# Page numbers of a paged cache: four by one register load, bounded once for the whole table

## The chip, the cores and the metric

The kernel runs on one core of a Trainium2 chip. The metric is the device time of one execution in microseconds (us). The profile is of one execution, taken by the hardware profiler; its engines are PE (TensorE matmuls), PEld (weight loads), DVE (VectorE), ACT (ScalarE), POOL (GpSimd) and SP (SyncE), and SP here computes nothing: it loads registers and issues DMAs, in the order of its own instruction stream.

## What the kernel computes

One inference step of a two-layer decoder trunk, for a prompt of 1,040 tokens and for 8 samples of 4 new tokens each. Layer 0 is a convolution module and a ConvFFN; then a shared latent key/value side is computed; layer 1 is multi-head latent attention and a ConvFFN. The part that matters here is the attention of the samples over a paged cache:

```python
page_table = jax.random.permutation(key, n_phys)[:n_used].reshape(DEC_BATCH, n_pages)   # (8, 16) int32, n_phys = 160

def step(carry, phys):                    # scanned over the 16 pages of every sample
    m, l, acc = carry
    c = cache_lat[phys]                   # (8, 128, 128): one page of each sample
    kr = cache_kr[phys]                   # (8, 128, 32)
    k = key_nope(c, w_uk, knorm_nope)     # rms_norm of c @ w_uk, per head
    s = (q_nope . k + q_rope . kr) * SM_SCALE
    ...                                   # running softmax over s, acc += p . c
```

So 128 pages are read, each at an address that depends on a number in `page_table`. The norms of the keys need `c @ w_uk` of every page too.

## The kernel before

The program is written out in full (no loops on the chip). A planner orders the instructions of each engine by simulated times of readiness and by priorities; inside `manual_schedule(engines={X})` the order in which the code emits the instructions of engine X is kept among themselves. All loads named below are issued by SP, whose instructions run one after another; a DMA whose buffer is not yet free holds back everything behind it on SP.

The cache is read twice, each time as 32 groups of four pages, by the helper `pages(pt, slot, moves)` (L569). For each of the four pages it loads one int32 of the table (`pt`, a tile of 1 x 128 in SBUF) into a register of SP with `value_load` (L573), which also emits a check of the number against 0 and 159, and then issues one DMA whose source address is computed from the register (L575). `between` and `more` let other DMAs (L348) be put behind single pages at the very start.

- `cache_open` and `cache_norms` (L580 to L632), from the start of the kernel on: the first 128 columns of each page (`ct`, 64 KB a page) are brought in, split in a high and a low part (`ch` on ACT, `cl` on DVE or POOL), multiplied by `w_uk` on PE (L616) and squared and summed, as filler between the matmuls of the convolution module. `ct` has two buffers of four pages. At the very start the eight `x` tiles of the residual stream (L348) are loaded between the pages; the first weights `raw<-pw` (L155) come later on the same queue.
- `latents` (L910 to L1057) opens the second part: it loads the table again (L927, L928).
- `samples` (L1453 to L1652): the attention of the samples, in four pairs of samples `sp` = 0 to 3. `scores(sp)` has `fetch` (L1528) bring in 8 groups of four pages of the pair (`pg`, 192 KB a page: latent transposed, latent, rope key), from two pools of 8 tiles that the pairs take in turn; it splits them on ACT and DVE (L134, L1558, L135, L1559), multiplies on PE (L150, L1573) and combines on DVE (L1575, L1579). `values(sp)` does the softmax on ACT (L1592), transposes (L1603) and multiplies with the pages (L1614). `values(sp)` and `scores(sp + 1)` are interleaved step by step (L1636 to L1642). Before each pair a tile of key norms, `rk`, comes on the same queue (L1539).
- The first pair's scores are worked between the matmuls of the prompt's attention (L1297 to L1330); the second pair's pages go to memory that the prompt's attention gives back at its end (L1330). After `samples` come `project` (L1654) and the second ConvFFN.

Of the kernel before, what the change touches and what calls it, by code (L numbers as in the profile page):

```python
# [11 lines left out]
I32 = mybir.dt.int32  # L12
ALU = mybir.AluOpType
# [95 lines left out]
class Pair:  # L109
    def __init__(self, pools, n=0):  # L110
        self.pools, self.n = pools, n
# [6 lines left out]
class Prog:  # L118
    def __init__(self, tc, a, o):
        self.tc, self.nc, self.a, self.o = tc, tc.nc, a, o  # L120
        self.gate, self.between, self.help, self.wedge = [], [], 0, []

    def pool(self, es, name, bufs, side="left", **k):
        return es.enter_context(self.tc.tile_pool(name=name, bufs=bufs, side=side, reuse_waits="tile", **k))
# [414 lines left out]
    def layer_norm(self, ys):  # L539
# [26 lines left out]
        with self.tc.high_priority(PRIO):  # L566
            return self.rows_rstd(t, sums, T0)

    def pages(self, pt, slot, moves):  # L569
        nc = self.nc  # L570
        with self.tc.manual_schedule(engines={nc.sync.engine}):
            for j in range(4):
                pg = nc.sync.value_load(pt[0:1, slot + j:slot + j + 1], min_val=0, max_val=159)  # L573
                for t, src in moves:
                    last = nc.sync.dma_start(t[:, j], src(bass.ds(pg, 1)))  # L575
                if self.between:
                    self.more(self.between.pop(0))
        return last

    def cache_open(self, es):  # L580
        nc, a = self.nc, self.a
        self.kp = kp = self.pool(es, "kp", 2, "right")
        k1 = self.pool(es, "k1", 1, "right")
        self.pk = self.pool(es, "pk", 2, "right", space=PSUM)
        self.ks = self.pool(es, "ks", KS, "right")
        raw = self.wp.tile([128, 1024], F32, name="raw")
        self.ukh, self.ukl = k1.tile([128, 1024], F32R, name="ukh"), k1.tile([128, 1024], F32R, name="ukl")
        nc.sync.dma_start(raw, a["wuk"])
        self.split(self.ukh, self.ukl, raw)
        self.pt = k1.tile([1, 128], I32, name="pt")  # L590
        nc.sync.dma_start(self.pt, a["pt"])
        self.ss = k1.tile([128, 128, H], F32, name="ss")
        self.fill, self.pks, self.halve = self.cache_norms(), [], HALVE
        self.on_pool = ()
# [315 lines left out]
    def latents(self, es, eq, xh, xl, sq):  # L910
        nc, a, o = self.nc, self.a, self.o
        ac = self.pool(es, "ac", 1, "right")
# [11 lines left out]
        self.qs = ac.tile([128, H, NS], F32, name="qs")  # L924
        self.kr8 = ac.tile([32, 64], F32, name="kr8")
        self.cn8 = ac.tile([64, CL], F32, name="cn8")
        self.pt = ac.tile([1, 128], I32, name="pt")  # L927
        nc.sync.dma_start(self.pt, a["pt"])  # L928
        tabs = {}
        cs = {n: self.cst(n).rearrange("p (a b) -> p a b", b=16) for n in ("cos", "sin")}  # L930
        with ExitStack() as e2:
# [923 lines left out]
```

## Time and profile before

| | us |
|---|---|
| median of 3 runs (lowest to highest) | 2805.16 (2804.45 to 2807.96) |
| the profiled execution | 2805.34 |
| its span (first to last instruction) | 2803.6 |

The span is what the trace covers; the profiled execution is 1.7 us longer than it. In the rows, L573 is line 573 of the kernel, `SPq` is SP's instruction stream, "x8" is a count, and a row of a timeline or a chain begins with its start and its duration in us. A row of the page's section on DMA issues ends with the KB of one DMA and the median us from issue to landing.

### The profile page before, as it was taken

To read this page: it belongs to the slowest core of one execution; us is meant where nothing else is said; L and a number is where in the kernel's file an instruction comes from. 1 tells how busy PE (TensorE), PEld (TensorE's weight loads), DVE (VectorE), ACT (ScalarE), POOL (GpSimd) and SP (SyncE) were. 2 spreads that over 40 slices of the span, in tenths; PEclk is the share of its full clock that TensorE was granted. 3 is DMA by queue.
4 is the path that set the end of the run, shared out by engine and by line. 5 is a ranking of instruction groups with operands and counts; after the bars stand their busy time and mean duration, and the time that the engine had idled before them with its cause. 6 is when DMAs were issued, how large, how long until landed. Compare 5 with 4: busy or idle time off the path is not lost.

```text
span 2803.6 us, 47232 instructions
## 1 busy us (share of the span) xinstructions
PE 2664.4 (95%) x16934; PEld 2451.2 (87%) x16934; DVE 1889.1 (67%) x3526; ACT 1357.2 (48%) x3730; POOL 680.4 (24%) x988
## 2 busy tenths in 40 slices
PE   7999996999999999999789999988999999999999
PEld 5888875999999999999667676655999999999999
DVE  8899996478888774144776867665468777776131
ACT  6777775345445452023655565555235445444020
POOL 1467661033333330001211212100004333331000
PEclk9999997999999999999999999977999999999999
DMA  4111110503222235132101001357402222227122
GB/s 137 56 41 57 54 38 16 178 25 101 86 94 87 84 127 207 42 102 77 39 8 34 16 20 54 93 159 234 163 32 72 84 82 72 87 80 264 40 86 75
DMA packets 127776, 238.29 MB, mean 85 GB/s; under 512 B 39778, under 2 KB 81140, under 8 KB 127412
## 3 DMA queue, kind: packets, MB, share of 16 engines
q1 hardware_dynamic: 103828, 200.82, 22.2%
q0 software_dynamic: 9600, 32.36, 3.1%
q10 hardware_dynamic: 14112, 2.09, 0.5%
q8 instruction: 133, 2.18, 0.3%
q14 instruction: 103, 0.84, 0.1%
HBM read 183.90 MB, written 51.31 MB: 84 GB/s over the span
## 4 chain that ended last, share of the span: by engine, by line
PE 83%; DVE 7%; ACT 4%; issue 2%; DMA 2%; SPq 2%; POOL 0%; ACTq 0%; DVEq 0%; POOLq 0%
PE ps L758 29%; PE ps L174 22%; PE pk L616 5%; PE g L410 4%; PE v L1297 4%; PE ps L807 3%; PE p L150 2%; PE ps L196 2%; PE ps L976 1%; PE p L1307 1%; PE p L1309 1%; PE p L1310 1%; PE s L1267 1%; PE ps L150 1%; PE po L1614 1%
## 5 line engine op out<-in xcount | busy, mean ns | idle before, releaser
L134 ACT ACTIVATE wh<-raw 128x512 fp32r<-128x512 f32 (+2 forms) x256 | 191.1, 750 | 543.0 <-PE ps L174 341.4
L135 DVE TENSOR_TENSOR wl<-raw,wh 128x512 fp32r<-128x512 f32 (+2 forms) x244 | 201.4, 828 | 109.1 <-ACT wh L134 103.1
L904 DVE TENSOR_TENSOR x<-ps,x 128x1074 f32<-128x1074 f32 (+1 forms) x48 | 61.0, 1270 | 289.7 <-PE ps L174 289.7
L728 DVE SCALAR_TENSOR_TENSOR c<-ub,c,c 128x1040 f32<-128x1040 f32 (+1 forms) x176 | 225.5, 1314 | 30.0 <-ACT c L725 29.2
L631 ACT ACTIVATE qq<-pk 128x64 f32<-128x64 f32 x760 | 164.4, 244 | 74.9 <-PE pk L616 74.9
L723 POOL COPY sb<-ub 128x32 f32<-128x32 f32 x88 | 88.2, 1005 | 403.4 <-DVE ub L769 364.8
L1297 PE MATMUL v<-pf,vf 128*128 128x512 f32 (+4 forms) x448 | 175.6, 475 | 9.7 <-ACT pf L1314 9.2
L625 POOL TENSOR_TENSOR sq<-sq 128x256 f32<-128x256 f32 (+3 forms) x234 | 141.2, 608 | 104.3 <-ACT sq L620 95.9
L631 ACT ACTIVATION_READ_ACCUMULATOR qq<-pk 128x1 f32 x760 | 159.8, 228 | 0.2
L1314 ACT ACTIVATE pf<-p 128x512 f32<-128x512 f32 (+4 forms) x224 | 99.6, 451 | 121.7 <-DVE p L1312 101.0
L508 DVE SCALAR_TENSOR_TENSOR a<-u,c,a 128x512 f32<-128x512 f32 x216 | 151.2, 751 | 6.1 <-ACT a L501 6.1
L174 PE MATMUL ps<-xh,wh 128*128 128x358 f32 (+1 forms) x672 | 147.7, 328 | 7.1 <-ACT xh L134 5.4
L174 PE MATMUL ps<-xl,wh 128*128 128x358 f32 (+1 forms) x672 | 147.4, 327 | 0.1
L174 PE MATMUL ps<-xh,wl 128*128 128x358 f32 (+1 forms) x672 | 147.4, 327 | 0.0
L174 PE MATMUL ps<-al,wh 128*128 128x358 f32 (+1 forms) x672 | 147.2, 327 | 0.0
L174 PE MATMUL ps<-ah,wl 128*128 128x358 f32 (+1 forms) x672 | 146.5, 326 | 0.0
L174 PE MATMUL ps<-ah,wh 128*128 128x358 f32 (+1 forms) x672 | 146.2, 326 | 0.0
L616 PE MATMUL pk<-ukh,ch 128*128 128x512 f32 x256 | 112.3, 439 | 27.3 <-ACT ch L134 14.0
L725 ACT ACTIVATE c<-ub,c 128x1074 f32<-128x1074 f32 (+1 forms) x88 | 101.3, 1185 | 66.3 <-DVE ub L769 53.1
L174 PEld LDWEIGHTS ps<-xh,wh 128*128 128x128 f32 x672 | 116.7, 190 | 10.4 <-ACT xh L134 6.3
L620 ACT ACTIVATE sq<-pk 128x512 f32<-128x512 f32 x161 | 98.2, 616 | 46.4 <-PE pk L616 43.6
L134 ACT ACTIVATE wh<-s 128x512 fp32r<-128x512 f32 x120 | 75.7, 630 | 92.9 <-PE ps L758 86.3
(588 smaller groups left out, 9093.0 us busy)
## 6 DMA issues: line engine op xcount, KB each, us to landing
raw<-wup SPq DMA_DIRECT2D x88, 512.0 KB, 3.5
pg<-ctn SPq DMA_DIRECT2D x128, 192.0 KB, 2.6
raw<-wdn SPq DMA_DIRECT2D x32, 448.0 KB, 3.3
raw<-pw SPq DMA_DIRECT2D x24, 512.0 KB, 3.7
d_a<-c POOLq DMA_DIRECT2D x22, 537.0 KB, 3.5
raw<-d_a SPq DMA_DIRECT2D x22, 537.0 KB, 4.8
d_a<-c POOLq DMA_DIRECT2D x22, 531.0 KB, 3.1
raw<-d_a SPq DMA_DIRECT2D x22, 531.0 KB, 5.1
```

The lines of the kernel that those rows point to most:

```text
L134: return (nc.scalar.activation(h, src, AF.Copy), (eng or nc.vector).tensor_tensor(out=l, in0=src, in1=h.bitcast(F32), op=ALU.subtract))
L135: (eng or nc.vector).tensor_tensor(out=l, in0=src, in1=h.bitcast(F32), op=ALU.subtract))
L174: nc.tensor.matmul(p[:, c, :ch], s[:, k * 128:(k + 1) * 128], m[k][:, off + c * ch:off + (c + 1) * ch], start=k == 0 and i == 0, stop=k == ...
L410: y = nc.tensor.matmul(p[:, 0], x[:, k * 128:(k + 1) * 128], m[k][:, t * ch:t * ch + ch], start=k == 0 and i == 0, stop=k == KD - 1 and i ...
L508: nc.vector.scalar_tensor_tensor(out=p[:, :ND] if j == n - 1 else acc, in0=x[:, j:j + ND], scalar=w[:, j:j + 1], in1=to if j == 1 else acc ...
L616: x = nc.tensor.matmul(ps, s[:, j, :], m[:, 512 * c:512 * c + 512], start=i == 0, stop=i == 2)
L625: nc.gpsimd.tensor_tensor(out=to, in0=v[:, :, :n], in1=v[:, :, n:2 * n], op=ALU.add)
L631: nc.scalar.activation(q, ps[:, 64 * h:64 * h + 64], AF.Square, accum_out=ss[:, p, 8 * c + h:8 * c + h + 1])
L725: x = nc.scalar.activation(c, ub, AF.Copy, scale=wd[:, t, 2:3])
L728: nc.vector.scalar_tensor_tensor(out=c[:, 2:pe], in0=ub[:, tap:tap + pe - 2], scalar=wd[:, t, tap:tap + 1], in1=c[:, 2:pe], op0=ALU.mult, ...
L758: nc.tensor.matmul(ps, w[:, s], m[:, lo:hi], start=first and k == 0 and i == 0, stop=k == KD // 2 - 1 and i == 2, skip_group_check=True)
L1297: nc.tensor.matmul(o[:, at_:], vf[:m, b, c], p[:m, :512 - at_], start=b == 0, stop=last)
```

## The change

The numbers of a group's four pages are brought into registers by one call, without a check on them; the whole table is bounded to 0..159 by one VectorE instruction when it has landed (`page_table`, at both places that load it); and the load of a group is ordered behind the last DMA of the group before it (`follow` sets an order on SP, not a wait).

```diff
+    def page_table(self, pool):
+        self.pt = pool.tile([1, 128], I32, name="pt")
+        self.nc.sync.dma_start(self.pt, self.a["pt"])
+        self.nc.vector.tensor_scalar(out=self.pt, in0=self.pt, scalar1=0, scalar2=159, op0=ALU.max, op1=ALU.min)
+
     def pages(self, pt, slot, moves):
         nc = self.nc
         with self.tc.manual_schedule(engines={nc.sync.engine}):
-            for j in range(4):
-                pg = nc.sync.value_load(pt[0:1, slot + j:slot + j + 1], min_val=0, max_val=159)
+            loads, at = nc.values_load_multi_w_load_instructions(pt[0:1, slot:slot + 4], [nc.sync.engine], min_val=0, max_val=159,
+                                                                skip_runtime_bounds_check_because="page_table() has bounded them")
+            for x in loads:
+                self.follow(x, self.paged)
+            for j, pg in enumerate(at):
                 for t, src in moves:
                     last = nc.sync.dma_start(t[:, j], src(bass.ds(pg, 1)))
                 if self.between:
                     self.more(self.between.pop(0))
+        self.paged = [last]
         return last
...
-        self.pt = k1.tile([1, 128], I32, name="pt")
-        nc.sync.dma_start(self.pt, a["pt"])
+        self.page_table(k1)
...
-        self.pt = ac.tile([1, 128], I32, name="pt")
-        nc.sync.dma_start(self.pt, a["pt"])
+        self.page_table(ac)
```

## Rows read from the trace of the kernel before

**Rows 1.** The profile's page: its span, the busy time of TensorE, the chain of work that ended last by engine, and one row of the DMA issues.

```profile
span 2803.6 us, 47232 instructions
...
PE 2664.4 (95%) x16934; PEld 2451.2 (87%) x16934; DVE 1889.1 (67%) x3526; ACT 1357.2 (48%) x3730; POOL 680.4 (24%) x988
...
PE 83%; DVE 7%; ACT 4%; issue 2%; DMA 2%; SPq 2%; POOL 0%; ACTq 0%; DVEq 0%; POOLq 0%
...
pg<-ctn SPq DMA_DIRECT2D x128, 192.0 KB, 2.6
```

**Rows 2.** The timeline of what SP issued from 1792 to 1940 us, merged: start, us until the end of the last issue, what, and how many.

```profile
1792.97 77.51 SPq L575 DMA_DIRECT2D pg<-ctn  x60
1870.53 0.42 SPq L1539 DMA_DIRECT2D rk<-d_ss  x1
1871.21 31.80 SPq L575 DMA_DIRECT2D pg<-ctn  x32
...
1903.74 31.39 SPq L575 DMA_DIRECT2D pg<-ctn  x32
1935.24 0.84 SPq L1479 DMA_DIRECT2D rx<-wuv  x2
```

**Rows 3.** The instructions of lines 573 and 575 from 1871 to 1903 us: operation, count, ns least/median/most, first and last start.

```profile
L573 SPq TENSOR_LOAD <-pt x24: 263/268/277, 1871.6 to 1901.9; - x24
L573 SPq FUSED_REGOPS  x24: 152/152/159, 1871.9 to 1902.3; - x24
...
L575 SPq DMA_DIRECT2D pg<-ctn x32: 332/333/808, 1871.2 to 1902.7; - x32
...
DMA to landing us min/median/max: 2.3/2.5/4.0
```

**Rows 4.** The chain of work that ended last, SP alone, from 1895 to 1903 us: the issues of three pages and what stands between the last two of them.

```profile
1898.77 0.33 SPq L575
...
1899.34 0.33 SPq L575
...
1899.72 0.27 SPq L573
1899.99 0.05 issue
1900.04 0.15 SPq L573
...
1900.44 0.33 SPq L575
```

**Rows 5.** Busy time by stretch: the second, third and fourth pair's fetch, what follows it, and ten microseconds inside the third pair. Columns: stretch, its us, busy us of each engine with the instructions counted, granted clock of TensorE, busy share of the DMA engines, GB/s.

```profile
1839.00:1871.00 32.00, 26.54 (x130) 18.84 (x131) 15.83 (x36) 17.07 (x39) 0.00 (x0) 0.77 0.67 200
1871.00:1903.50 32.50, 28.76 (x145) 20.46 (x143) 19.64 (x46) 17.94 (x41) 0.00 (x0) 0.81 0.68 202
1903.50:1935.20 31.70, 28.57 (x142) 20.52 (x141) 18.81 (x44) 18.21 (x41) 0.00 (x0) 0.78 0.68 205
1935.20:1957.50 22.30, 16.82 (x91) 13.40 (x92) 8.32 (x18) 11.13 (x24) 0.00 (x0) 0.69 0.76 277
1885.00:1895.00 10.00, 10.00 (x74) 8.18 (x72) 6.25 (x15) 6.26 (x17) 0.00 (x0) 1.00 0.66 190
```

**Rows 6.** The timeline of all engines around 1834 to 1840 us, where the prompt's attention ends and the second pair's fetch begins.

```profile
1833.68 0.59 ACT L1324 ACTIVATE l<-v 64x512 f32<-64x512 f32 x1
...
1834.34 3.34 DVE L1329 RECIPROCAL l<-l 128x512 f32<-128x512 f32 x1
...
1838.15 0.69 DVE L1330 TENSOR_TENSOR o<-o,l 128x512 f32<-128x512 f32 x1
...
1839.03 10.69 SPq L575 DMA_DIRECT2D pg<-ctn  x11
```

**Rows 7.** Line 573 from 1300 to 1335 us, columns as in the third group.

```profile
L573 SPq TENSOR_LOAD <-pt x32: 263/266/788, 1308.2 to 1326.4; - x32
```

**Rows 8.** The timeline of all engines from the start to 45 us: the second instruction of DVE in the kernel's own work, and a small VectorE instruction of the kind that the change adds.

```profile
6.20 1.23 DVE L135 TENSOR_TENSOR ukl<-raw,ukh 128x1024 fp32r<-128x1024 f32 x1 [5.20 <-ACT ukh L134]
...
27.46 0.16 DVE L254 TENSOR_SCALAR nr_v<-ps 128x9 f32<-128x9 f32 x1
```

**Rows 9.** Busy time by stretch near the start, columns as in the fifth group.

```profile
2.00:6.00 4.00, 0.00 (x0) 0.00 (x0) 0.00 (x0) 0.91 (x2) 0.00 (x0) 1.00 0.98 307
6.00:10.00 4.00, 0.00 (x0) 0.00 (x0) 1.23 (x1) 2.16 (x3) 0.00 (x0) 1.00 0.99 367
...
34.00:38.00 4.00, 3.30 (x16) 2.12 (x15) 3.15 (x7) 3.81 (x8) 1.79 (x3) 1.00 0.57 175
```

**Rows 10.** The chain of work that ended last, from the start to 60 us.

```profile
2.14 2.66 DMA pt<-pt
...
25.73 0.33 SPq L575
...
34.01 0.33 SPq L575
34.39 3.50 DMA raw<-pw
...
39.92 1.13 DVE wl L135
```

**Rows 11.** What SP waited for, over the whole span: line that waits, engine and tile that released it, us in total, times, longest.

```profile
SPq L575 <- POOL cl L135: 151.6, 23, 10.4
```

More of the change, by code (lines that the diff above doesn't have):

```diff
@@ L120, in __init__ @@
         self.tc, self.nc, self.a, self.o = tc, tc.nc, a, o
-        self.gate, self.between, self.help, self.wedge = [], [], 0, []
+        self.gate, self.between, self.help, self.wedge, self.paged = [], [], 0, [], []
     def pool(self, es, name, bufs, side="left", **k):
```

## The prediction

> **What bounds the kernel now.** I read the page first: TensorE is busy for 95% of the span, and SP's stream makes up 2% of the chain that ended last, some 56 us [rows 1]. A change to SP alone can hardly win more than that, and it is worth something only where SP is the last to be ready. So I looked for the stretch in which those 2% lie. The timeline of SP's issues shows it: from 1839.03 us [rows 6] to 1935.24 us [rows 2] SP issues pages with no gap, 96.2 us for three pairs, one pair in 31.4 to 31.8 us plus its `rk`. In the same stretches PE is busy for 26.5 to 28.8 us of 32 at a mean granted clock of 0.77 to 0.81, DVE for 16 to 20, ACT for 17 to 18, and the DMA engines for 0.67 to 0.68 of the time [rows 5]. None of them is full; a page lands 2.5 us after its issue in the median [rows 3], so no queue of transfers stands before it. What runs without a pause is SP's stream, and this is the bound of that stage. Before 1839 the stage can't begin: the second pair's memory comes free with DVE's L1330, behind a RECIPROCAL of 3.34 us that itself waits for the last values of the prompt's attention [rows 6].
>
> **The price of a page on SP.** In the chain [rows 4], the end of one page's issue to the end of the next is 1.10 us where the number is loaded in between (1899.67 to 1900.77), and 0.57 us where it is not (1899.10 to 1899.67; this one also has the wait for the group's buffer). So load and check cost 0.53 to 0.59 us. The load with the gap behind it is 0.32 of this, the rest, 0.21 to 0.27, is the check (its first instruction alone is 0.15). A group now has three loads in its stream, since the planner has drawn the group's first load ahead: 24 loads for 32 pages [rows 3], and the 32 missing ones stand together at 1308 to 1326 us [rows 7]. A group is then 0.57 + 3 x 1.10 = 3.87 us, eight are 31.0, with 0.68 for `rk` (1870.53 to 1871.21 [rows 2]) 31.6: what the timeline shows within 3%.
>
> **What the change does to it.** The checks go: 3 x 0.24 us a group. The three loads become one, which `follow` now pins into the stream, so nothing is drawn ahead any more. No row shows a load of four numbers. It costs at least what a load of one costs, 0.27 us, and I see no reason for more than four of them, 1.07 us. Nor does a row tell whether it is one instruction or four; four are the upper end again, but for three gaps of 0.05. A group is then 4 x 0.54 + 0.32 = 2.5 us, or 4 x 0.54 + 1.07 + 0.05 = 3.3 us, and a pair with its `rk` 20.5 or 27.0 us of SP. I take the lower end, since one load is an access to a row of 16 neighbouring bytes and its 268 ns vary by 14 ns only [rows 3], which looks like a round trip.
>
> The Trainium skill, "Runtime: NRT & Kernel Launch", section on instruction fetch mechanics, says that a register load costs about 200 ns for each register, even in bulk; that is told of loads from HBM, and no run here shows it for SBUF. By it a load of four would be about 0.8 us, an estimate from that page, and a pair 24.7 us on SP: near PE's figure below, so that the sum would stay, and rival (a) would be cut to 2784 us. "DMA: Bandwidth & Descriptors", section on latency and other measured facts, gives a floor of about 600 ns for such a load; the trace disagrees, with 268 ns for one number.
>
> **What is late next.** With SP at 20.5 us a pair, others take over. DMA: 32 x 192 KB [rows 1] and 256 KB of `rk` are 6.55 MB; 202 GB/s at a share of 0.68 makes 297 at full share, so 22.1 us. (The start shows 307 to 367 GB/s at 0.98 to 0.99 [rows 9], with longer rows.) PE: ten microseconds fully busy at clock 1.00 hold 74 matmuls [rows 5]; the 142 to 145 of a pair are 19.4 us so, and at the mean clock of 0.78 that these pairs were granted, 25 us. DVE 19 to 20, ACT 18. So PE at the present mixed clock is the next bound, and I add 0.5 us for hand-overs between engines that are all 70% busy or more: 25.5 us a pair. Three pairs: 96.2 - 76.5 = 19.7 us won. What follows the last page, 22.3 us to 1957.5 [rows 5], is values and weights and stays.
>
> **The other places.** The first pair's pages (28 from 1793 on) come some 10 us earlier, but the prompt's attention sets the end of that stretch [rows 6]: 0. In the convolution module SP waits for `cl`, 151.6 us in 23 waits [rows 11]; a faster SP waits longer: 0. The cover there is PE's own work. The 32 loads at 1308 us vanish from a time at which nothing waits for SP: 0. Near the start SP is on the chain from 25.73 to 34.39 us [rows 10], two groups and two weight loads, 8.7 us; at 2.5 us a group the second `raw<-pw` leaves 2.8 us earlier. DVE, which must still make `wl` and the rest, idled 0.85 us of 34 to 38 [rows 9], so between 0.85 and 2.8; I take the lower.
>
> **What it adds.** One TENSOR_SCALAR on DVE, twice. The nearest row is 0.16 us for 128 x 9 [rows 8]; with two semaphores 0.3. Lower bound 0. At 1304 us it lies beside matmuls. At the start SP's first load now waits for it, and behind that load stand the remaining `x` tiles and all pages. If DVE's stream has it behind the subtraction `ukl`, which ends at 7.43 us [rows 8], the load comes at 7.6 us, 2.8 us late against the 4.8 of now (2.14 + 2.66 [rows 10]). The DMA engines are 98 to 99% busy from 2 to 10 us [rows 9], with what was issued before; that hides most of it, and the next two groups give back 2.8. Between 0 and 2.8; I take 0.3, since the planner places by readiness: it drew 32 loads ahead as soon as the table was there [rows 7].
>
> **The sum.** 2805.3 (profiled execution; the median, 2805.16, is 0.2 lower) - 19.7 - 0.85 + 0.3 = 2785 us.
>
> **Rivals.** (a) The clock follows the work. PE's waits for pages shrink, it is granted full clock, and PE needs 19.4 us; DMA is then the bound with 22.1 and 0.4 for hand-overs, 22.5. For it: the stretch with PE fully busy has clock 1.00 [rows 5]. 3 x 22.5 = 67.5, that is 28.7 won, 2776 us. (b) The load grows with the registers it fills, 4 x 0.27: SP stays the bound with 27.0 a pair, 81 us, 15.2 won, 2790 us. Against it the steady 268 ns. The page on the runtime named above speaks for this one. (c) Other engines are nearer to their limits than busy shares tell: their buffers and order (three PSUM tiles for two products, softmax behind the last score) make 30 us a pair: 6 won, 2799 us. (d) SP wasn't the bound, or the call still checks each number in the stream: within 0.2% of before. The gapless issue speaks against it. (e) The other side: shorter, more frequent waits keep PE at its half clock throughout. Place: 1839 to 1935. A pair is then 2 x 19.4 = 38.8 us, 3 x 38.8 - 96.2 = +20, 2825 us. It decides from a mean clock under 19.4 / 32.1 = 0.60; the pairs now stand at 0.77 to 0.81, with more waiting than will be left, which speaks against it.
>
> **How the numbers follow.** The forecast 0.47, (a) 0.20, (b) 0.13, (c) 0.10, (d) 0.05, (e) 0.05. 0.2% is 5.6 us, about what a measurement of this kernel can tell from no change. The forecast, (a), (b) and most of (c) are faster; a tenth of it and (d) are the same; (e) is slower, with a little for an order that the planner changes elsewhere: 0.87, 0.07, 0.06. The range takes in (a) with the upper end at the start (2773) and (c) (2799); outside lie (d), (e) and the tails. The forecast's own range is 2780 to 2790.
>
> **What would show it.** Right: SP's issues of a pair take 20 to 27 us; L573 has one TENSOR_LOAD for four pages near 0.3 us and no FUSED_REGOPS; from 1839 on PE is busy for over 90% with a clock above 0.8; the stage ends about 20 us earlier, and all after it is shifted by this. Wrong: a load of 0.8 us or more, pages that land later than 4 us (DMA), a clock at 0.6, or the second pair's fetch not beginning near 1839.

## The result and the profile after

The changed kernel takes 2776.96 us (median of 4 runs, 2774.47 to 2778.64); the kernel before, run beside it on the same chip, takes 2806.19 us (2804.45 to 2807.96). The ratio is 0.9895, with a 95% interval of 0.9878 to 0.9912: 29 us faster. The prediction said 2785 us, some 20 faster, with 2773 to 2799 as the range.

The page of the profile after, the lines that answer to [rows 1]:

```profile
span 2774.8 us, 46538 instructions
...
PE 2644.7 (95%) x16934; PEld 2443.1 (88%) x16934; DVE 1888.5 (68%) x3528; ACT 1354.7 (49%) x3730; POOL 664.5 (24%) x988
...
PE 85%; DVE 7%; ACT 3%; issue 2%; DMA 2%; SPq 1%; POOL 0%; ACTq 0%; DVEq 0%
...
pg<-ctn SPq DMA_DIRECT2D x128, 192.0 KB, 3.9
```

The span is 28.8 us shorter with the same 16934 matmuls. SP's part of the chain went from 2% to 1%. The last line is the first sign of a new limit: a page of the samples now lands 3.9 us after its issue, where it was 2.6.

Where the 28.8 us lie is seen by following a few marked instructions through both traces (end of each, us from the start of the span):

| | before | after | shift |
|---|---|---|---|
| last gate product of the convolution module (PE, `g`) | 386.0 | 382.4 | -3.6 |
| end of the prompt's attention (DVE, `o`, L1330, after L1337) | 1838.8 | 1833.7 | -5.1 |
| last values of the samples (PE, `po`, L1614, after L1621) | 1958.9 | 1927.7 | -31.2 |
| end of the span | 2803.6 | 2774.8 | -28.8 |

So the samples' stage, from the end of the prompt's attention to the last values (from here on "the stage"), went from 120.0 to 94.0 us: 26 of the 29. Some 5 us lie before it, 3.6 of them in the convolution module, and some 2.4 were given back behind it. Only the stage and the 3.6 us are shown to come from the change. The mark at the attention's end moves by a few us between kernels that differ little up to there (1833.7 here, 1837.2 with smaller pages in the same kernel), and from the last values to the end it is 844.7 us before and 847.1 after, but 847.1 and 847.6 too in two of the kernels below that fetch the samples' pages the old way.

The stage first. SP's issues after, as in [rows 2] (the page's DMA is now L583, the load L577):

```profile
1787.73 66.64 SPq L583 DMA_DIRECT2D pg<-ctn  x60
1854.43 0.42 SPq L1546 DMA_DIRECT2D rk<-d_ss  x1
1855.45 20.89 SPq L583 DMA_DIRECT2D pg<-ctn  x32
1876.44 0.37 SPq L1546 DMA_DIRECT2D rk<-d_ss  x1
1877.41 19.86 SPq L583 DMA_DIRECT2D pg<-ctn  x32
```

A pair's pages take 20 to 21 us of SP where they took 31.4 to 31.8. The instructions of the two lines, as in [rows 3], from 1850 (L577) and 1855 (L583) to 1900 us: operation, count, ns least/median/most, first and last start.

```profile
L577 SPq TENSOR_LOAD <-pt x17: 294/300/304, 1852.0 to 1894.8; - x17
...
L583 SPq FUSED_REGOPS  x64: 37/37/42, 1855.2 to 1896.8; - x64
L583 SPq MOVE pg<-ctn x64: 29/29/29, 1855.4 to 1896.9; - x64
L583 SPq DMA_DIRECT2D pg<-ctn x64: 332/333/1493, 1855.4 to 1896.9; - x64
...
DMA to landing us min/median/max: 3.1/4.0/5.2
```

One load brings four numbers in 0.300 us, one number took 0.268. The check has gone from L577; what stands between the pages is the work on the address, 37 and 29 ns, and gaps. The longest issue is now 1.49 us, not 0.81, and a page lands in 4.0 us: SP now and then runs into the transfers.

Busy time by stretch, columns as in [rows 5]: of before, the fetch and what follows the last page; then the same two stretches of after, and the three pairs' fetches of after.

```profile
1838.80:1935.20 96.40, 83.86 (x414) 59.81 (x414) 54.45 (x128) 53.22 (x121) 0.00 (x0) 0.79 0.68 202
1935.20:1958.90 23.70, 18.19 (x100) 14.36 (x100) 9.38 (x19) 11.64 (x25) 0.00 (x0) 0.71 0.74 265
```

```profile
1833.70:1897.30 63.60, 59.51 (x320) 45.49 (x321) 44.42 (x105) 43.55 (x100) 0.00 (x0) 0.84 0.93 299
1897.30:1927.70 30.40, 28.03 (x196) 23.46 (x194) 15.30 (x36) 18.99 (x46) 0.00 (x0) 0.94 0.59 209
...
1833.80:1855.40 21.60, 20.79 (x124) 15.55 (x124) 11.33 (x25) 14.52 (x34) 0.00 (x0) 0.93 0.89 282
1855.40:1877.40 22.00, 20.23 (x100) 15.40 (x99) 18.92 (x45) 15.64 (x36) 0.00 (x0) 0.77 0.95 306
1877.40:1897.30 19.90, 18.50 (x100) 14.54 (x99) 14.14 (x36) 13.29 (x32) 0.00 (x0) 0.83 0.95 310
```

This is the main reading of the case. The matmul counts of the stage are the same, 514 and 516. The fetch became 33 us shorter, but only 320 of them are done when it ends, where 414 were; the other 196 fill the stretch behind the last page, which grew from 23.7 to 30.4 us. In that stretch TensorE is granted 0.94 of its 2.4 GHz (0.71 before). The DMA engines went from 0.68 to 0.93 of the fetch.

The chain of work that ended last says the same. Before, SP's issues of pages come back on it up to 1934.79 us, almost the last page. After, the last transfer of a page on it is the one issued at 1854.05 us, at the end of the second pair's fetch; from there to 1925 us it is TensorE, with pieces of DVE and ACT. The line of before, then those of after:

```profile
1934.79 0.33 SPq L575
```

```profile
1854.05 4.33 DMA pg<-ctn
1858.48 0.64 ACT ch L134
...
1859.17 2.94 PE sn L150 x9
```

The chain after the stage shows what was given back: the first long wait behind the samples, of before, then of after.

```profile
1957.46 3.36 DMA raw<-wo
```

```profile
1925.25 5.03 DMA x<-d_o
```

Before, `project` waits for its first weights, whose DMA was done at 1960.8, 1.9 us behind the last values. After, it is a tile of the attention's output, whose DMA took 5.0 us and was done at 1930.3, 2.6 us behind them, and which ACT has to split ahead of the weights. In the timeline of PE the first long run of products then starts 6.3 us behind the last values (1933.98 against 1927.69), where it was 4.3. That the change did this is not shown: in the two kernels below whose samples are fetched the old way, the same start comes 4.3 us (the new way for the key norms alone) and 6.0 us (smaller pages) behind the last values.

Near the start, busy time of the stretch up to the first gate product of the loop (the matmuls of the key norms alone, L616 and L624) and of the first round of the loop (all), before and after in turn:

```profile
0.00:83.20 83.20, 37.09 (x123) 23.47 (x123) 1.00 0.38 124
...
83.20:130.00 46.80, 45.68 (x232) 39.52 (x233) 44.51 (x77) 35.19 (x208) 25.62 (x34) 1.00 0.18 52
```

```profile
0.00:82.80 82.80, 38.52 (x132) 23.69 (x132) 1.00 0.38 128
...
82.80:126.60 43.80, 43.31 (x223) 38.16 (x224) 43.47 (x73) 32.72 (x205) 25.63 (x34) 1.00 0.17 50
```

Nine key-norm matmuls more are done before the loop, in a stretch in which PE is busy for 63 of 83 us; they are missing in the first round, in which PE is busy for 98 to 99%. That round is 3.0 us shorter. The first load of the table itself came later, at 5.54 us instead of 4.82: DVE's bounding took 0.215 us and stood in front of it. The first four `raw<-pw`, which SP issued at 30.0, 34.4 [rows 10], 36.3 and 43.0 us before, now go out at 14.9, 16.2, 26.3 and 28.7.

### The profile page after: what moved, and what is told of

The parts are those of the page before. It is cut to its first block, busy times and chain, and to the rows that moved or that the text cites. A ratio compares the mean times of both kernels' runs of the same rounds, so it can differ in the third digit from the quotient of the medians.

```text
span 2774.8 us, 46538 instructions
## 1 busy us (share of the span) xinstructions
PE 2644.7 (95%) x16934; PEld 2443.1 (88%) x16934; DVE 1888.5 (68%) x3528; ACT 1354.7 (49%) x3730; POOL 664.5 (24%) x988
## 4 chain that ended last, share of the span: by engine, by line
PE 85%; DVE 7%; ACT 3%; issue 2%; DMA 2%; SPq 1%; POOL 0%; ACTq 0%; DVEq 0%
PE ps L766 29%; PE ps L174 24%; PE pk L624 5%; PE g L410 5%; PE v L1304 4%; PE ps L815 3%; PE ps L196 2%; PE p L150 2%; PE ps L983 1%; PE p L1314 1%; PE p L1316 1%; PE p L1317 1%; PE s L1274 1%; DVE a L508 1%; PE sn L150 1%
## 5 line engine op out<-in xcount | busy, mean ns | idle before, releaser
L731 POOL COPY sb<-ub 128x32 f32<-128x32 f32 x88 | 69.0, 786 | 414.1 <-DVE ub L777 367.8
L633 POOL TENSOR_TENSOR sq<-sq 128x256 f32<-128x256 f32 (+4 forms) x234 | 143.0, 615 | 96.6 <-ACT sq L628 88.2
L624 PE MATMUL pk<-ukh,ch 128*128 128x512 f32 x256 | 110.9, 434 | 25.6 <-ACT ch L134 13.8
```

The costliest lines, as they stand in the source:

```text
L624: x = nc.tensor.matmul(ps, s[:, j, :], m[:, 512 * c:512 * c + 512], start=i == 0, stop=i == 2)
L633: nc.gpsimd.tensor_tensor(out=to, in0=v[:, :, :n], in1=v[:, :, n:2 * n], op=ALU.add)
```

## Experiments

"Stage" below is as above, "fetch" the lengths of the second, third and fourth pair's fetch (from a pair's first page to the next pair's first, so with `rk`; the last pair's to the end of its last issue), each from the trace; before they are 120.0 and 32.2, 32.5, 31.4 us, after 94.0 and 21.5, 22.0, 19.9. Where the samples are worked alike, the stage repeats within 0.8 us: 120.0 and 120.8 in two kernels the old way, 94.0, 94.0 and 93.3 in three the new way. Ratios are to the kernel before, run beside each.

### The check and the load, one at a time

**The four-number load, with the check of each number kept.** The call's own check is left on:

```diff
-            loads, at = nc.values_load_multi_w_load_instructions(..., skip_runtime_bounds_check_because="page_table() has bounded them")
+            loads, at = nc.values_load_multi_w_load_instructions(...)
```

> The changed kernel with the check of each number kept in SP's stream (one load of four, bounded table, order as changed). Theory: SP's time for a page sets the stage of the samples; with 0.24 us for each check a group is 0.30 + 0.05 + 4 x (0.54 + 0.24) = 3.5 us, a pair with its rk 28.5 us against 32.1 before and 21.5 changed, so about 11 us of the 29 remain, and little of the gain in the convolution module: 2790 to 2797 us. Rival (the gain came from another order that the planner chose, or from TensorE's clock, not from SP's time): near the changed kernel, 2775 to 2780 us.

Measured: 2794.4 us, ratio 0.9958 (0.9941 to 0.9974); fetch 30.0, 29.6, 27.4; stage 110.2. The line of the load in the third pair:

```profile
L577 SPq FUSED_REGOPS  x28: 147/150/155, 1868.4 to 1891.2; - x28
L577 SPq SEQ_ASSERT  x28: 18/18/18, 1868.6 to 1891.4; - x28
L577 SPq TENSOR_LOAD <-pt x7: 295/298/302, 1868.1 to 1890.1; - x7
```

**One load for each page, without the check.**

```diff
-            loads, at = nc.values_load_multi_w_load_instructions(pt[0:1, slot:slot + 4], ...)
-            for j, pg in enumerate(at):
+            for j in range(4):
+                loads, (pg,) = nc.values_load_multi_w_load_instructions(pt[0:1, slot + j:slot + j + 1], ...)
```

> The changed kernel with one load for each page, none of them checked in the stream, and each ordered behind the DMA before it. Theory: a group is 4 x (0.27 + 0.05 + 0.54) = 3.4 us, a pair with its rk 28.2 us: 2790 to 2797 us, that is, the loads saved are worth about as much as the checks saved. Rival: near the changed kernel, 2775 to 2780 us, if the checks alone or the order made the gain.

Measured: 2791.17 us, ratio 0.9954 (0.9938 to 0.9971); fetch 28.5, 28.0, 27.4; stage 107.6. Each edit alone brings the last pair's fetch from 31.4 to 27.4, both together to 19.9, and the stage follows each time: 120.0, 110.2 and 107.6, 94.0. Seen from the changed kernel each is worth 7.5 us a pair. Seen from the kernel before it is 4.0, since there 8 of 32 loads with their checks had been drawn ahead [rows 3, 7] and in these two nothing is. That is what a stage bound by SP's stream does.

### One stage at a time

**The new way for the samples alone**; the key norms keep the old loop.

```diff
+    def pages_old(self, pt, slot, moves):      # the loop of before
...
-            self.pages(self.pt, 4 * g, ...)         # cache_norms
+            self.pages_old(self.pt, 4 * g, ...)
```

> The new way of loading for the pages of the samples alone; the pages for the key norms as before, with a check and a load each and an unbounded table. Theory: the two places add up; this one holds the gain between 1834 and 1958 us of the trace, 26 us, less the 2.4 us that come back behind it: 2780 to 2784 us. Rival (the 5 us that were already there at 1834 us come from the samples' part too, by the planner's order): 2775 to 2779 us.

Measured: 2777.75 us, ratio 0.9899 (0.9882 to 0.9915); fetch 21.5, 21.9, 20.5; stage 94.0. The time is below the 2780 to 2784 that were expected and in the rival's range. The trace is against the rival as far as the convolution module goes: the last gate product stands 0.05 us from where it was before, so nothing is won there. The attention's end comes 2.1 us earlier than before, which is within what that mark moves by.

**The new way for the key norms alone**; the samples' `fetch` calls the old loop.

> The new way of loading for the pages of the key norms alone, in the convolution module; the samples' pages as before. Theory: 4 to 5 us faster than before, 2800 to 2803 us, most of it between 83 and 386 us where the trace of the changed kernel gained 3.2 us. Rival: within 2 us of before.

Measured: 2800.81 us, ratio 0.9986 (0.9977 to 0.9996); stage 120.8, the last gate product 3.9 us earlier. So the two gains are separate: 26 us from the samples, some 3 to 4 from the norms.

### Whose limit was it, whose is it now

**Pages of two thirds, after** (the rope keys are not read; the latent stands in for them):

```diff
-[(pg, lambda p: a["ctn"][p].rearrange("a p n -> p (a n)"))]
+[(pg[:, :, 0:256], lambda p: a["ctn"][p].rearrange("a p n -> p (a n)")[:, 0:256])]
...
-                        kr = pg[:96, :, 256:384]
+                        kr = pg[:96, :, 128:256]
```

> The changed kernel with pages of the samples of 128 KB instead of 192 KB; the rope part of the page is left out of the load, and the rope product takes the latent part in its place (so that part of the computation is changed; all engines do as much work as before). Theory: the fetch of the changed kernel runs at the DMA engines' limit (0.95 busy, 306 GB/s). With two thirds of the bytes SP's stream is the limit, 8 x 2.43 + 0.7 = 20.1 us a pair against 21.5, so the fetch of three pairs ends 3 to 5 us earlier, the DMA share falls to about 0.7; but TensorE, busy for 83 of 90 us there, passes on only a part: 2772 to 2777 us. Rival (SP is still the bound after the change): the fetch stays at 21 to 22 us a pair and the time the same, 2775 to 2779 us.

**The same edit on the kernel before.**

> The same cut of the pages of the samples to 128 KB in the kernel before (rope part left out of the load, latent part in its place in the rope product). Theory: before the change SP's stream is the bound, so a third less bytes changes nothing: 32 us a pair as before, DMA share 0.45 in place of 0.68, time within 4 us of before. Rival (the DMA engines or the landing of pages were the bound): 10 us or more faster.

Measured: on the kernel before, 2807.47 us, ratio 1.0005 (0.9992 to 1.0017), fetch 32.2, 32.4, 31.4, stage 118.2; on the changed kernel 2780.51 us, ratio 0.992 (0.9904 to 0.9937), fetch 21.3, 21.1, 20.3, stage 91.1. Busy time of the third pair's fetch, before and after, both with two thirds of the bytes:

```profile
1872.70:1904.40 31.70, 28.43 (x143) 20.53 (x141) 19.48 (x45) 17.85 (x41) 0.00 (x0) 0.77 0.48 140
```

```profile
1858.70:1878.70 20.00, 18.60 (x85) 14.39 (x85) 16.73 (x39) 13.53 (x30) 0.00 (x0) 0.68 0.71 211
```

In the kernel before the fetch does not notice that a third of the bytes is gone: the DMA share falls from 0.68 to 0.48 and the fetch stays (the stage is 1.8 us shorter, the time no different). This settles that SP, not the transfers, set its pace. In the changed kernel the share falls from 0.95 to 0.71 and the fetch is a microsecond a pair shorter at most, 0.6 us over the three. That is about what the rival expected, 21 to 22 us a pair with SP still the bound: the transfers alone do not set it either, SP's stream stands just below them. The stage is 3 us shorter in the profiled execution, but the median is no better than the changed kernel's (its runs lie between 2774.5 and 2783.2): the gain that was expected did not come.

**No order on the load.** The planner may draw loads ahead again:

```diff
-            for x in loads:
-                self.follow(x, self.paged)
```

> The changed kernel without the order of a group's load behind the group before it; the planner may draw loads ahead, as it did with 32 of them before the change. Theory: at most 0.35 us a group goes out of SP's stream, 2.8 us a pair, and as the DMA engines are the limit the time stays: 2774 to 2779 us. Rival (SP is still the bound): 6 to 8 us faster, 2768 to 2771 us; slower if loads drawn ahead get in the way of other DMAs.

Measured: 2776.03 us, ratio 0.9899 (0.9882 to 0.9915); fetch 21.0, 21.8, 21.0; stage 93.3; no load was drawn ahead. The order costs and gives nothing; what loads drawn ahead would have done, this run does not test.

**Sixteen numbers by one load** in the samples, two loads a pair instead of eight.

```diff
+            if at is None:
+                loads, at = nc.values_load_multi_w_load_instructions(pt[0:1, slot:slot + n], ...)     # n = 16
```

> The changed kernel with the numbers of all sixteen pages of a sample brought in by one load, at its first group, in the part for the samples; the key norms keep four. Theory: a load of four took 0.300 us against 0.268 of one, 11 ns for each further register, so a load of sixteen takes about 0.43 us and SP saves 6 x 0.35 - 2 x 0.13 = 1.8 us a pair; the DMA engines are the limit, so the time stays, 2774 to 2779 us. Rival (SP is still the bound): 4 to 6 us faster, 2770 to 2773 us.

Measured: 2775.86 us, ratio 0.9907 (0.9885 to 0.9929); fetch 21.2, 20.9, 18.2; stage 93.2. The load's line from 1830 to 1900 us:

```profile
L578 SPq TENSOR_LOAD <-pt x5: 968/973/987, 1835.2 to 1877.3; - x5
```

The load of sixteen takes 0.973 us, not the 0.43 that I had drawn through one and four. Two of them are 1.95 us a pair against 8 x 0.300 = 2.4: SP was relieved by little. Even so the three fetches took 60.3 us together instead of 63.3, a second sign that SP's stream still paces the fetch, while the stage became only 0.8 us shorter. The next run relieves SP by far more.

**One DMA for two pages**, 16 issues a pair instead of 32. The second page is the neighbour of the first in the cache, so other data is read.

```diff
+            for j in (0, 2):
+                last = nc.sync.dma_start(t[:, j:j + 2, 0:n], self.a["ctn"][bass.ds(at[j], 2)].rearrange("a p n -> p a n")[:, :, 0:n])
```

> The changed kernel with one DMA of 384 KB for two pages of the samples: it brings the first page's physical neighbour in place of the second page (so another page is read there; the table is bounded to 158). SP has half the issues, the bytes and the work of all other engines stay. Theory (SP and the DMA engines are both at their limit near 21 us a pair in the changed kernel): SP's stream falls to about 12 us a pair, the DMA engines go on at 306 to 325 GB/s, so a pair still takes 20 to 21.5 us and the time stays at 2773 to 2778 us. Rival (SP alone is the bound; cutting bytes changed nothing): a pair in 15 us or less, 2765 us or less.

**The same with two thirds of each page**, so that SP and the transfers are both relieved.

> As the run before, and only two thirds of each page are loaded (the rope part is left out, the latent part stands in its place in the product): SP and the DMA engines are both relieved, the other engines work as before. Theory: the fetch runs ahead, 14 to 16 us a pair where buffers are free, and what is left is TensorE with its hand-overs; its 486 matmuls of the stage take 66 us at the rate of a full clock, and the stage of 94 us becomes 84 to 89 us: 2766 to 2772 us. Rival (TensorE and the chain of the softmax already set the stage in the changed kernel): 2774 to 2778 us.

Measured: 2772.67 us, ratio 0.9889 (0.9873 to 0.9906), stage 89.7 with whole pages; 2782.73 us, ratio 0.9913 (0.9895 to 0.9931), stage 92.8 with two thirds. Busy time of the first of them: the three fetches, and from the last page to the last values.

```profile
1836.40:1851.60 15.20, 13.81 (x76) 9.17 (x75) 7.74 (x17) 7.19 (x20) 0.00 (x0) 0.91 0.97 317
1851.60:1872.60 21.00, 18.74 (x63) 13.12 (x62) 18.29 (x39) 14.44 (x29) 0.00 (x0) 0.58 1.07 374
1872.60:1886.50 13.90, 13.90 (x99) 11.53 (x97) 11.48 (x27) 10.16 (x23) 0.00 (x0) 1.00 1.06 370
1886.50:1925.90 39.40, 37.12 (x240) 30.77 (x240) 22.10 (x55) 25.69 (x64) 0.00 (x0) 0.91 0.58 203
```

The 20 to 21.5 us a pair that were expected of it were wrong: two pairs took 15.2 and 13.9 us, and the transfers went to 370 GB/s and more. The fetch is over at 50 us where it took 63 after the change, and 240 matmuls are left behind the last page instead of 196: 13 us less of fetch gave 4 us of stage (by one trace each; in the ratios, 0.9889 and 0.9895, the two kernels can't be told apart). The fetch has stopped being the bound. SP now waits for buffers that TensorE's values still hold, for 0.9 us in all after the change, here with whole pages (where 5.0 us more go in short waits for the transfers) and then with two thirds. The line that waits, what it waits for, us in total, times, longest:

```profile
SPq L597 <- PE po L1633: 4.7, 3, 3.2
```

```profile
SPq L597 <- PE po L1633: 13.8, 4, 10.1
```

With two thirds of the bytes the stage even stood at 92.8, so relieving SP and the DMA queues was worth 1 to 4 us of the stage in these two traces, and the 84 to 89 us of stage and 2766 to 2772 of time expected of the second were wrong. (That run also lost 9 us behind the stage: its last values come 31.4 us earlier than before, its end 22.6. This isn't explained, and its time says little for that reason.)

**One of the three score products left out** (`mm3` multiplies high by high, high by low and low by high; here the low part of the query is dropped), on the changed kernel. TensorE has some 1.9 us a pair less to do.

```diff
-                    self.mm3(sn[:, :w], qth[:, sm], qtl[:, sm], cc[e][0], cc[e][1], ...)
+                    nc.tensor.matmul(sn[:, :w], qth[:, sm], cc[e][0], ...)
+                    nc.tensor.matmul(sn[:, :w], qth[:, sm], cc[e][1], ...)
```

> The changed kernel with two of the three products of the samples' scores (the one with the low part of the query is left out), 1.9 us less of TensorE a pair at full clock; loads and transfers as changed. Theory (the fetch sets the stage): time as the changed kernel, 2773 to 2778 us. Rival (TensorE sets it): 4 to 8 us faster, 2768 to 2772 us.

**Two pages by one DMA, and only the first of the three products.**

> Here all three suspects are relieved at once: one DMA for two pages (the second page is the neighbour of the first, so other data; the table is bounded to 158) as in the two-by-one kernel, and of the three products of a score with the latent only the first is left, 16 matmuls a pair fewer, about 3.8 us a pair at full clock or 11 us from the attention's end on. The two-by-one kernel's stage (end of the prompt's attention to the end of the last values) was 89.7 us. If TensorE's work is what sets the stage now, it falls to 77 to 83 us, and the time to 2757 to 2766. If the hand-over between the pairs (softmax behind the last score, then transposes, then values) sets it, with PE waiting longer in it, the stage stays at 87 to 91 us and the time at 2766 to 2774, the rest of the gain lying before the attention's end.

Measured: 2770.55 us, ratio 0.9877 (0.9861 to 0.9894), stage 92.6 with two products; 2769.86 us, ratio 0.9873 (0.9851 to 0.9894), stage 85.2 with all relieved. Busy time of the latter, stretches as above, and its longest wait of the stage:

```profile
1838.60:1852.70 14.10, 11.17 (x68) 7.72 (x66) 7.02 (x17) 7.38 (x20) 0.00 (x0) 0.91 0.99 334
1852.70:1872.20 19.50, 13.56 (x41) 8.32 (x42) 17.10 (x39) 12.91 (x26) 0.00 (x0) 0.54 1.07 374
1872.20:1886.50 14.30, 13.62 (x97) 11.01 (x95) 13.63 (x31) 11.77 (x29) 0.00 (x0) 1.00 1.07 375
1886.50:1923.60 37.10, 32.96 (x208) 26.26 (x208) 22.14 (x54) 25.94 (x61) 0.00 (x0) 0.86 0.64 227
```

```profile
PEld sn L1592 <- DVE kh L1578: 11.5, 10, 2.4
```

With two products the time lies in the range of the rival, by which TensorE sets the stage (2768 to 2772). But of the 5.5 us by which its trace is shorter than that of the changed kernel only 1.4 lie in the stage, little more than the 0.8 by which the stage repeats; 2.2 lie before it and 1.9 behind. With all relieved, 85.2 lies between the two theories, 77 to 83 if TensorE's work sets the stage and 87 to 91 if the hand-over between pairs does; the time lies in the range of the second, 2766 to 2774. The work taken away can be estimated: busy us times granted clock, summed over the four rows, is 71.1 us with three products (2.4 GHz would do it in about that time) and 59.5 with one, 11.6 less. The stage became 4.5 us shorter. With two products it was 1.4 shorter for 3 x 1.9 = 5.7 less. So TensorE's work counted for a quarter to two fifths of its size, by one trace each. The longest waits are now on DVE, which splits the rope keys (`kh`) and is busy for 17.1 of 19.5 us in the stretch where TensorE's clock is at 0.54. Which of DVE's splits or the hand-over is the larger part, no run here tells apart.

## Why the prediction was right or wrong, step by step

**SP's stream bounds the stage, and where it ends: right.** The one-edit-at-a-time runs and the lost third of the bytes show it, the latter without any effect on the fetch of the kernel before.

**The prices on SP: right.** The load of four is 0.300 us, the lower of the two bounds (0.27 to 1.07). A pair needs 20.5 us by the sum with its `rk`; 21.5 and 22.0 were taken, and 19.9 by the last pair without it. Rival (b), 1.07 us for a load of four, falls. The estimate made from the Trainium skill, "Runtime: NRT & Kernel Launch", section on instruction fetch mechanics (about 0.8 us for four, told of loads from HBM), does not hold for four numbers in SBUF, where the run has 0.300 us.

**What is late next: the step that failed.** I had 25.5 us a pair, TensorE's 142 to 145 matmuls at the mixed clock of before, as if a pair's fetch could not end before its matmuls do. The fetch takes 21.1 us a pair, 63.3 in all. SP's own 20 us and the DMA engines, busy for 0.93 of it, both stand there, SP's stream a little nearer, as the runs with fewer bytes and with sixteen numbers show, by one trace each. For the DMA engines this is the bound of rival (a) (22.5 us), a little faster, since in two of the three pairs they moved 306 to 310 GB/s. But the other half of (a), full clock and a TensorE that keeps up, is not what came: the clock was 0.84, and TensorE fell behind. The fetch and the matmuls are coupled only through the buffers of two pairs, and these let TensorE lag by some 96 matmuls; SP's waits for these buffers, 0.9 us after the change, grew to 4.7 and 13.8 only where the fetch was made faster still.

**"What follows the last page stays": wrong, by 6.7 us.** It is here that the lag was paid, 30.4 us instead of 23.7 (the 22.3 of the prediction end 1.4 us before the last values do). Taken together, 32.8 - 6.7 = 26 us were won in the stage where 19.7 stood in the sum; the two steps were off in opposite directions. Taking the stage as a whole shows the room that was there: by an estimate from the rows above (busy time times granted clock) its matmuls are 66.2 + 12.9 = 79 us at full clock before, 50.0 + 28.0 x 0.94 = 76 after, less than 80 of the 120 us. That is a lower bound, not a forecast: the stage came to 94.0, between it and the 100.3 of the sum.

**That rival (a)'s 2776 us were met is luck.** Its fetch of 67.5 us was 4 too long, and it left out the 6.7 us of the tail, the 5 before the stage and the 2.4 behind it, which nearly cancel.

**The clock, as rival (e) had it: excluded.** ACT's waits for `pg` in the stage fell from 25.0 to 15.5 us, and the clock rose in both stretches, from 0.79 to 0.84 and from 0.71 to 0.94. Rival (d) falls with it, and (c), 30 us a pair, too.

**The convolution module at nothing: mis-sized, 3 to 4 us.** "The cover there is PE's own work" is true from the loop's beginning on, but SP decides how much of the key-norm work is done before it, in 83 us in which PE has 20 to spare. Nine more matmuls there and one gap of 0.99 us less (PE waited at 88.02 us of before) are about the 3.0 us of the first round. That the norms' pages are the cause is shown by the two one-stage runs (-3.9 and -0.05 us); that it comes by these nine matmuls is read from the counts, not tried. I had put the start's gain on the second `raw<-pw`, 0.85 us: the planner moved that load up by 18 us, the others by 10 to 15, and the first gate product came 0.37 us earlier.

**The bounding on VectorE: right at near zero.** It took 0.215 us and delayed SP's first load by 0.72, behind which nothing is seen to be late.

**What lies behind the stage: open.** Some 2.4 us were not passed on, 2.0 of them in `project`, which in this trace is released by a transfer that was hidden before. Since kernels with the old fetch lose as much there, it can't be put down to the change.

The forecast's own range, 2780 to 2790, did not hold the time; the wide one did, since rival (a) had drawn its lower end. One of the signs of being wrong, pages that land later than 4 us, stood at its edge: the median was 4.0, the longest 5.2.

## What to carry to other kernels

When the stream of a DMA-issuing engine has no gap for many microseconds while all others do, each instruction in it costs its full duration: here 24 checks of 0.24 us and 24 loads of 0.32 us, by the prediction's prices, made 13 of the 31 us of a pair, and its eight loads of four put less than 3 back. When such a bound is lifted, do not price the stage by the next engine's work within one step of the loop; buffers let the consumers lag, so sum each engine's work over the whole stage, its tail included, as a lower bound, and ask what is issued behind it. And look for the same code elsewhere: where it fills a warm-up, a faster stream can move work out of the stretch that is full.

## What the runs showed of the hardware that was not expected

- A register load on SP from SBUF: one number 0.268 us, four 0.300, sixteen 0.973. It is neither flat nor a fixed price for each.
- DMAs of 384 KB brought 370 to 375 GB/s over the third and fourth pair's fetch (317 and 334 over the second's), with a share of busy time that the profile gives as 1.06 to 1.07; single pages of 192 KB stood at 306 to 310 GB/s at 0.95.
- In the kernels with two pages by one DMA, TensorE's granted clock was 0.54 and 0.58 over the middle fetch, most of it 1.2 GHz, where it was busy for 13.6 of 19.5 and 18.7 of 21.0 us and DVE for 17.1 and 18.3; in the 14 us behind it, busy for 95 to 100%, it had 1.00, that is 2.4 GHz.
